# Decay sums of a state-space branch: clamped differences per head on VectorE and ScalarE, in place of two GpSimd passes and two VectorE passes

## The chip, the cores and the metric

The kernel runs on one core of a Trainium2 chip. The metric is the device time of one execution in microseconds (us); less is better. The core's engines each work through a queue of their own in order: TensorE (PE in the profile, with PEld for its weight loads), VectorE (DVE), ScalarE (ACT), GpSimd (POOL) and SyncE (SP), which issues the transfers of the weights. An instruction whose semaphore has not come holds up everything behind it on its engine, and nothing else.

## The reference, cut to what matters

The layer has a half-step feed-forward block, then two mixers side by side (a chunked state-space branch and a sparse attention branch), a memory cross-attention and a second half-step feed-forward block, for 256 tokens of 1024 features in float32. The change is in the state-space branch. With l = 128 tokens in a chunk, two chunks and 16 heads it computes

```
def segsum(a):
    l = a.shape[-1]
    cs = jnp.cumsum(a, axis=-1)
    diff = cs[..., :, None] - cs[..., None, :]
    mask = jnp.tril(jnp.ones((l, l), dtype=bool))
    return jnp.where(mask, diff, -jnp.inf)
...
    a = (dt * a_head.reshape(g, r)).transpose(0, 3, 4, 1, 2)
    decay_in = jnp.exp(segsum(a))
    cb = jnp.einsum('bclgn,bcsgn->bcgls', cmat, bmat)
    y_diag = jnp.einsum('bcgls,bgrcls,bcsgrp->bclgrp', cb, decay_in, xdt)
```

Since a is negative, a difference that survives the mask is at most 0. The kernel clamps every difference to at most 0, takes the exponential, and zeroes what the mask drops.

## The kernel before

**Tiles.** `E[tb]`, one for each chunk `tb`, holds for every head h the 128 x 128 differences: partition s, column (h, l), so 128 partitions x 2048 columns. `cs` holds the running sums, one column for each chunk and head. Products are made in a split float32 form: each piece of weights (128 x 1024) comes by a transfer of SyncE into one of 4 buffers `raw`, ScalarE writes its rounded high half `whi` (L150), and VectorE, for some pieces GpSimd, writes the rest `wlo` (L151); both have 6 buffers, so a cast waits until TensorE is done with the piece six before.

**Making E.** `ssd_decay` gets the sums with one small product (L548), turns them over (L555), writes them to DRAM (L560) and reads them back to all partitions with two transfers from GpSimd's queue (L562). GpSimd then subtracts `cs` from the whole of `E[tb]` (L563). Later, in `ssd`, VectorE clamps the whole of `E[tb]` to at most 0 (L599), ScalarE takes the exponential in halves of 8 heads (L604), VectorE multiplies by the masked products of C and B (L606), and TensorE uses the result as weights (L622).

**What runs beside it.** `fly` (L122) weaves generators together by counting TensorE's work: `ssd_decay`, `latent`, `xbc` and `k_index` share the first stretch. `xbc` (L433) makes 8 units of two 128-column blocks: TensorE fills a PSUM bank `ps_mm` from two weight pieces, ScalarE starts a block (L454), VectorE adds three shifted products (L456, "the convolution" below), ScalarE applies the silu (L458), and for the units that come last TensorE turns the block `wa` over (L120) into a bank `ps_t`, which ScalarE copies out (L443). The turns stand in TensorE's queue between the products, so a late silu stops all the products behind it. `k_index` turns over the index keys as well; ScalarE and VectorE split them into `kidxh` and `kidxl`. The second stretch weaves `dsa` (L653), `ssd` and `fill_mixers`; in it `dsa` adds up the index scores in `acc` on VectorE (L695).

**What sets the order.** The order on each engine is laid down when the program is built, by a scheduler that goes by its own estimates of the durations and may move an instruction ahead of others that wait; `issue_after` holds some instructions back behind a named one. Nothing is reordered on the chip.

Of the kernel before, what the change touches and what calls it, by code (L numbers as in the profile page):

```python
# [21 lines left out]
AF = mybir.ActivationFunctionType  # L22
ALU = mybir.AluOpType
AX = mybir.AxisListType

P = 128
T = 256
NTB = 2
# [4 lines left out]
H = 16  # L33
# [17 lines left out]
class Layer:  # L51
# [481 lines left out]

    def ssd_decay(self):

        nc = self.nc
        hb = lambda i: self.hv[:, None, i * H:(i + 1) * H].to_broadcast([P, NTB, H])
        dt = self.dtr
        nc.vector.tensor_tensor(dt, dt, hb(0), op=ALU.add)
        self.softplus(dt.rearrange("p a b -> p (a b)"), NTB * H)  # L540
        ea = self.small([P, H], "ea", bufs=1)
        nc.scalar.activation(ea, self.hv[:, H:2 * H], AF.Exp)
        dA = self.small([P, NTB, H], "dA", bufs=1)
        nc.vector.scalar_tensor_tensor(dA, dt, -1.0, ea[:, None, :].to_broadcast([P, NTB, H]),
                                       op0=ALU.mult, op1=ALU.mult)
        yield 14.0
        csp = self.psum("t")[:, :NTB * H]
        self.mm(csp, self.triu, dA.rearrange("p a b -> p (a b)"))  # L548
        cs = self.cs = self.small([P, NTB, H], "cs", bufs=1)
        nc.vector.tensor_copy(cs, csp.rearrange("p (a b) -> p a b", b=H))  # L550
        yield 1.5
        csT_p = self.psum("t")
        csT = self.small([P, T], "wa", bufs=4)[:H].rearrange("p (a b) -> p a b", b=P)
        for tb in range(NTB):
            self.transpose(csT_p[:H, tb * P:(tb + 1) * P], cs[:, tb, :])  # L555
        nc.vector.tensor_copy(csT, csT_p[:H, :T].rearrange("p (a b) -> p a b", b=P))
        scr = self.dp.tile([NTB, H * P], F32, name="cs_rows")
        self.E = []
        for tb in range(NTB):
            nc.gpsimd.dma_start(scr[tb].rearrange("(h l) -> h l", l=P), csT[:, tb, :])  # L560
            e = self.big((7, 9)[tb], F32, (P, H, P), "E")
            nc.gpsimd.dma_start(e.rearrange("p h l -> p (h l)"), scr[tb].partition_broadcast(P))  # L562
            nc.gpsimd.tensor_tensor(e, e, cs[:, tb, :].unsqueeze(2).to_broadcast([P, H, P]), op=ALU.subtract)  # L563
            self.E.append(e)

    def ssd(self, zs, xtok, bc, yT):

        nc = self.nc
        cs, E, dt, dskip = self.cs, self.E, self.dtr, self.hv[:, 2 * H:3 * H]
# [2 lines left out]
        S0, xe = sx[:, 0, :], sx[:, 1, :]  # L572
        dte, ecs = (self.small([P, H], tag, bufs=1) for tag in ("dte", "ecs"))
        with self.tc.issue_after(self.last_silu.ins):
            nc.scalar.activation(dte, E[0][:, :, P - 1], AF.Exp)
            nc.scalar.activation(ecs, cs[:, 1, :], AF.Exp)
        bcast = lambda v, n: v.unsqueeze(2).to_broadcast([P, n, HD])
        hview = lambda v: v.rearrange("p (h d) -> p h d", d=HD)
# [11 lines left out]
        for tb in range(NTB):  # L590
            ts = slice(tb * P, (tb + 1) * P)
            e = E[tb]
            cb = self.psum("t").rearrange("p (g c) -> p g c", c=P)
            for g in range(G):
                self.mm(cb[:, g, :], bc[:, g, ts], bc[:, 4 + g, ts])
            cbm = self.small([P, G, P], "w2b", bufs=2)
            nc.vector.tensor_tensor(cbm, cb, self.triu[:, None, :].to_broadcast([P, G, P]), op=ALU.mult)
            with self.tc.issue_after(self.last_conv.ins):
                nc.vector.tensor_scalar(e, e, 0.0, None, op0=ALU.min)  # L599
            yield 0.0  # L600
            for half in range(2):
                hs = slice(half * 8, half * 8 + 8)
                with self.tc.issue_after(self.last_silu.ins):
                    nc.scalar.activation(e[:, hs, :], e[:, hs, :], AF.Exp)  # L604
                ev = e[:, hs, :].rearrange("p (g r) l -> p g r l", g=2)
                nc.vector.tensor_tensor(ev, ev, cbm[:, 2 * half:2 * half + 2, :].unsqueeze(2).to_broadcast(  # L606
                    [P, 2, H // G, P]), op=ALU.mult)
            yield SSD_US[tb]
# [6 lines left out]
        for tb in range(NTB):  # L615
            ts = slice(tb * P, (tb + 1) * P)
            e, yt = E[tb], xtok[:, tb, :]
            for half in range(2):
# [6 lines left out]
                if tb == 1:  # L625
                    po = self.psum("mm")
                    for g in (2 * half, 2 * half + 1):
# [3 lines left out]
                                            op=ALU.mult)  # L631
# [9 lines left out]
            for g in range(G):  # L641
                nc.scalar.activation(yt[:, g * 256:(g + 1) * 256], yt[:, g * 256:(g + 1) * 256], AF.Copy,
                                     scale=rs[:, g:g + 1])
# [434 lines left out]
```

## Time and profile before

| | |
|---|---|
| median of 3 runs | 815.67 us (815.64 to 818.44) |
| the profiled execution: its own time | 814.78 us |
| its span, first to last instruction | 812.9 us |
| TensorE (PE) busy | 789.4 us, 97% of the span |
| VectorE (DVE) busy | 592.4 us, 73% |
| ScalarE (ACT) busy | 448.4 us, 55% |
| GpSimd (POOL) busy | 68.2 us, 8% |
| mean granted TensorE clock | 0.988 |

TensorE is busy nearly all the time, so a time can change in two ways only: by the stretches in which TensorE waits, and by those in which it runs at the lower of its two clocks (1.2 in place of 2.4 GHz, shown as a granted clock of 0.5). The shares of the other engines are means over stages of different kinds and tell little: it matters where they are late for TensorE.

### The profile page before, as it was taken

To read this page: it belongs to the slowest core of one execution; us is meant where nothing else is said; L and a number is where in the kernel's file an instruction comes from. 1 tells how busy PE (TensorE), PEld (TensorE's weight loads), DVE (VectorE), ACT (ScalarE), POOL (GpSimd) and SP (SyncE) were. 2 spreads that over 40 slices of the span, in tenths; PEclk is the share of its full clock that TensorE was granted. 3 is DMA by queue.
4 is the path that set the end of the run, shared out by engine and by line. 5 is a ranking of instruction groups with operands and counts; after the bars stand their busy time and mean duration, and the time that the engine had idled before them with its cause. 6 is when DMAs were issued, how large, how long until landed. Compare 5 with 4: busy or idle time off the path is not lost.

```text
span 812.9 us, 13145 instructions
## 1 busy us (share of the span) xinstructions
PE 789.4 (97%) x5070; PEld 717.5 (88%) x5070; DVE 592.4 (73%) x960; ACT 448.4 (55%) x782; POOL 68.2 (8%) x69
## 2 busy tenths in 40 slices
PE   8999999999989998989999999999999999999996
PEld 5888888887889997989999998899988988888885
DVE  4868776448588989698889767965659777776445
ACT  5756565433476684477667644544444666565330
POOL 1100000000032451230000000200002000000000
PEclk9999999999999999799999999999999999999999
DMA  7876555553656621236444456574433755555531
GB/s 249 271 267 224 193 182 194 187 200 104 210 189 228 208 74 51 81 108 233 165 150 135 158 175 215 170 276 161 156 120 134 256 191 195 192 184 194 192 105 53
DMA packets 39919, 142.90 MB, mean 176 GB/s; under 512 B 4592, under 2 KB 4896, under 8 KB 39472
## 3 DMA queue, kind: packets, MB, share of 16 engines
q1 hardware_dynamic: 38016, 134.63, 49.4%
q0 software_dynamic: 1840, 7.43, 2.9%
q8 instruction: 40, 0.66, 0.3%
q14 instruction: 23, 0.19, 0.1%
HBM read 140.97 MB, written 1.06 MB: 175 GB/s over the span
## 4 chain that ended last, share of the span: by engine, by line
PE 74%; DVE 11%; issue 8%; ACT 4%; DMA 2%; POOL 1%; SPq 0%; DVEq 0%; ACTq 0%; POOLq 0%
PE ps_mm L116 69%; DVE wlo L151 3%; PE ps_t L116 2%; PE ps_t L120 2%; DMA raw<-in_ffn_in_dram 2%; ACT whi L150 1%; PE ps_s L116 1%; DVE acc L695 1%; DVE acc L702 1%; DVE wa L456 1%; DVE m L701 1%; DMA raw<-in_w_pssd_dram 0%; POOL rstd L289 0%; DVE kv L794 0%; DVE kv L793 0%
## 5 line engine op out<-in xcount | busy, mean ns | idle before, releaser
L151 DVE TENSOR_TENSOR wlo<-raw,whi 128x1024 fp32r<-128x1024 f32 (+2 forms) x245 | 301.0, 1231 | 129.1 <-ACT whi L150 125.1
L150 ACT CAST whi<-raw 128x1024 fp32r<-128x1024 f32 (+2 forms) x253 | 263.2, 1044 | 188.1 <-PE ps_mm L116 124.6
L116 PE MATMUL ps_mm<-x1T,whi 128*128 128x256 f32 x768 | 143.9, 288 | 0.0
L116 PE MATMUL ps_mm<-x0T,whi 128*128 128x512 f32 x352 | 123.7, 400 | 2.9 <-ACT whi L150 2.1
L116 PEld LDWEIGHTS ps_mm<-x1T,whi 128*128 128x128 f32 x768 | 122.3, 195 | 0.0
L116 PE MATMUL ps_mm<-x1T,wlo 128*128 128x256 f32 x384 | 110.2, 287 | 0.0
L116 PE MATMUL ps_mm<-x3T,whi 128*128 128x512 f32 x304 | 105.6, 392 | 0.0
L116 PE MATMUL ps_mm<-x0T,wlo 128*128 128x256 f32 x352 | 97.0, 282 | 0.3 <-DVE wlo L151 0.3
L116 PE MATMUL ps_mm<-x3T,wlo 128*128 128x256 f32 x304 | 85.1, 280 | 0.0
L116 PEld LDWEIGHTS ps_mm<-x0T,whi 128*128 128x128 f32 x352 | 65.8, 188 | 20.6 <-ACT whi L150 3.6
L116 PEld LDWEIGHTS ps_mm<-x1T,wlo 128*128 128x128 f32 x384 | 75.1, 195 | 0.0
L116 PEld LDWEIGHTS ps_mm<-x3T,whi 128*128 128x128 f32 x304 | 56.9, 187 | 12.4
L116 PEld LDWEIGHTS ps_mm<-x0T,wlo 128*128 128x128 f32 x352 | 65.7, 189 | 1.6 <-DVE wlo L151 1.4
L116 PE MATMUL ps_mm<-whi,ah 128*128 128x512 f32 x154 | 60.2, 391 | 0.0
L116 PE MATMUL ps_mm<-wlo,ah 128*128 128x512 f32 x154 | 60.1, 390 | 0.0
L116 PE MATMUL ps_mm<-whi,al 128*128 128x512 f32 x154 | 59.9, 389 | 0.0
L116 PEld LDWEIGHTS ps_mm<-x3T,wlo 128*128 128x128 f32 x304 | 57.5, 189 | 0.0
L289 POOL TENSOR_TENSOR rstd<-rstd,mhalf 128x1 f32<-128x1 f32 (+1 forms) x12 | 11.3, 941 | 537.0 <-DVE rstd L288 537.0
L177 DVE TENSOR_TENSOR wa<-wa,ps_mm 128x256 f32<-128x256 f32 x82 | 34.0, 418 | 30.2 <-ACT wa L176 30.1
L347 ACT ACTIVATE wa<-wa 128x256 f32<-128x256 f32 x41 | 17.1, 417 | 48.1 <-DVE wa L177 48.1
L116 PEld LDWEIGHTS ps_mm<-whi,al 128*128 128x128 f32 x154 | 28.9, 188 | 6.2
L116 PEld LDWEIGHTS ps_mm<-whi,ah 128*128 128x128 f32 x154 | 29.0, 188 | 5.6
(296 smaller groups left out, 1551.5 us busy)
## 6 DMA issues: line engine op xcount, KB each, us to landing
raw<-in_ffn_in_dram SPq DMA_DIRECT2D x87, 512.0 KB, 4.1
raw<-in_ffn_out_dram SPq DMA_DIRECT2D x44, 512.0 KB, 3.5
raw<-in_w_xbc_dram SPq DMA_DIRECT2D x16, 512.0 KB, 4.3
raw<-in_w_gate_dram SPq DMA_DIRECT2D x16, 512.0 KB, 3.4
raw<-in_w_z_dram SPq DMA_DIRECT2D x8, 512.0 KB, 3.6
raw<-in_w_qidx_dram SPq DMA_DIRECT2D x8, 512.0 KB, 3.9
raw<-in_w_q_dram SPq DMA_DIRECT2D x8, 512.0 KB, 3.5
raw<-in_w_pssd_dram SPq DMA_DIRECT2D x8, 512.0 KB, 4.6
```

The costliest lines, as they stand in the source:

```text
L116: self.nc.tensor.matmul(out, a, b, start=start, stop=stop)
L120: self.nc.tensor.transpose(out, in_, self.ident)
L150: self.nc.scalar.copy(hi, src)
L151: (engine or self.nc.vector).tensor_sub(lo, src, hi.bitcast(F32))
L177: self.nc.vector.tensor_add(out, out, ps[:, :T])
L289: self.nc.gpsimd.tensor_tensor(v, v, self.mhalf[:, :n], op=ALU.pow)
L347: nc.scalar.activation(sg, self.join(gate, sg), AF.Silu)
L456: self.last_conv = nc.vector.scalar_tensor_tensor(v[:, d:], src[:, :T - d], cw[:, 3 - d:4 - d], v[:, d:], op0=ALU.mult, op1=ALU.add)
L695: nc.vector.scalar_tensor_tensor(acc[:, s], rl[:, s], self.widx[:, tb, h:h + 1], prev[:, s], op0=ALU.mult, op1=ALU.add)
L701: nc.vector.max(m8, acc[:, s])
L702: nc.vector.match_replace(out=acc[:, s], in_to_replace=m8, in_values=acc[:, s], imm_value=KILL)
```

## The change

The two GpSimd passes over E (L563) and the two VectorE clamps over E (L599) go. In their place each head of each chunk gets an instruction of its own over 128 columns: heads 0 to 7 on VectorE, as subtract and minimum in one; heads 8 to 15 on ScalarE, as relu(cs - E), which is the clamped difference with its sign turned. The exponentials of the second half of the heads therefore take the scale -1, and `dte` is made by two small instructions in place of one. The generator waits 12 us of counted TensorE work after the transfers and then issues the 32 instructions.

```
             nc.gpsimd.dma_start(e.rearrange("p h l -> p (h l)"), scr[tb].partition_broadcast(P))
-            nc.gpsimd.tensor_tensor(e, e, cs[:, tb, :].unsqueeze(2).to_broadcast([P, H, P]), op=ALU.subtract)
             self.E.append(e)
+        yield 12.0
+        for tb in range(NTB):
+            for h in range(H // 2):
+                nc.vector.tensor_scalar(self.E[tb][:, h, :], self.E[tb][:, h, :], cs[:, tb, h:h + 1], 0.0,
+                                        op0=ALU.subtract, op1=ALU.min)
+            for h in range(H // 2, H):
+                nc.scalar.activation(self.E[tb][:, h, :], self.E[tb][:, h, :], AF.Relu, scale=-1.0,
+                                     bias=cs[:, tb, h:h + 1])
+            yield 6.0
...
-            nc.scalar.activation(dte, E[0][:, :, P - 1], AF.Exp)
+            for half in range(2):
+                hs = slice(half * 8, half * 8 + 8)
+                nc.scalar.activation(dte[:, hs], E[0][:, hs, P - 1], AF.Exp, scale=(1.0, -1.0)[half])
...
-            with self.tc.issue_after(self.last_conv.ins):
-                nc.vector.tensor_scalar(e, e, 0.0, None, op0=ALU.min)
...
-                    nc.scalar.activation(e[:, hs, :], e[:, hs, :], AF.Exp)
+                    nc.scalar.activation(e[:, hs, :], e[:, hs, :], AF.Exp, scale=(1.0, -1.0)[half])
```

Buffer numbers shift between the two programs: `wa_2517` and `wa_2523` of before are `wa_2515` and `wa_2521` of the change, `whi_2691` with its `wlo_2692` is `whi_2705` with `wlo_2706`, and E's chunks are `E_2415` (first) and `E_2419` or `E_2418` (second).

**VectorE, in the middle of `xbc`.** Before, the convolution of two blocks with a weight split between and behind them:

```order
L456 SCALAR_TENSOR_TENSOR wa_2517<-ps_mm_2456,feat,wa_2517 128x255
L456 SCALAR_TENSOR_TENSOR wa_2517<-ps_mm_2456,feat,wa_2517 128x254
L456 SCALAR_TENSOR_TENSOR wa_2517<-ps_mm_2456,feat,wa_2517 128x253
L151 TENSOR_TENSOR wlo_2795<-raw_2793,whi_2794 128x1024
L456 SCALAR_TENSOR_TENSOR wa_2523<-ps_mm_2456,feat,wa_2523 128x255
L456 SCALAR_TENSOR_TENSOR wa_2523<-ps_mm_2456,feat,wa_2523 128x254
L456 SCALAR_TENSOR_TENSOR wa_2523<-ps_mm_2456,feat,wa_2523 128x253
```

The same place in the changed program, where two more rows of E stand a few rows ahead, among the last two rows of the convolution of `bcT_2097`:

```order
L456 SCALAR_TENSOR_TENSOR wa_2515<-ps_mm_2454,feat,wa_2515 128x255
L568 TENSOR_SCALAR E_2415<-E_2415,cs_2352 128x128
L456 SCALAR_TENSOR_TENSOR wa_2515<-ps_mm_2454,feat,wa_2515 128x254
L568 TENSOR_SCALAR E_2415<-E_2415,cs_2352 128x128
L456 SCALAR_TENSOR_TENSOR wa_2515<-ps_mm_2454,feat,wa_2515 128x253
L568 TENSOR_SCALAR E_2415<-E_2415,cs_2352 128x128 x4
L568 TENSOR_SCALAR E_2418<-E_2418,cs_2352 128x128 x6
L456 SCALAR_TENSOR_TENSOR wa_2521<-ps_mm_2454,feat,wa_2521 128x255
L568 TENSOR_SCALAR E_2418<-E_2418,cs_2352 128x128
L456 SCALAR_TENSOR_TENSOR wa_2521<-ps_mm_2454,feat,wa_2521 128x254
L568 TENSOR_SCALAR E_2418<-E_2418,cs_2352 128x128
L456 SCALAR_TENSOR_TENSOR wa_2521<-ps_mm_2454,feat,wa_2521 128x253
```

All 16 rows of E on VectorE stand ahead of the last convolution row of `wa_2521`, and the weight splits that stood here have moved behind them.

**ScalarE, at the same place.** Before:

```order
L454 ACTIVATE bcT_2097<-ps_mm_2371,feat 128x256
L150 CAST whi_2691<-raw_2690 128x1024
L454 ACTIVATE wa_2517<-ps_mm_2456,feat 128x256
L458 ACTIVATE bcT_2097<-bcT_2097 128x256
L150 CAST whi_2794<-raw_2793 128x1024
L458 ACTIVATE wa_2517<-wa_2517 128x256
L454 ACTIVATE wa_2523<-ps_mm_2456,feat 128x256
L150 CAST whi_2800<-raw_2799 128x1024
L454 ACTIVATE wa_2590<-ps_mm_2529,feat 128x256
L458 ACTIVATE wa_2523<-wa_2523 128x256
```

In the changed program:

```order
L571 ACTIVATE E_2415<-E_2415,cs_2352 128x128 x2
L454 ACTIVATE wa_2515<-ps_mm_2454,feat 128x256
L571 ACTIVATE E_2415<-E_2415,cs_2352 128x128 x2
L458 ACTIVATE bcT_2097<-bcT_2097 128x256
L571 ACTIVATE E_2415<-E_2415,cs_2352 128x128 x4
L150 CAST whi_2705<-raw_2704 128x1024
L458 ACTIVATE wa_2515<-wa_2515 128x256
L454 ACTIVATE wa_2521<-ps_mm_2454,feat 128x256
L571 ACTIVATE E_2418<-E_2418,cs_2352 128x128 x5
L454 ACTIVATE wa_2604<-ps_mm_2527,feat 128x256
L571 ACTIVATE E_2418<-E_2418,cs_2352 128x128
L458 ACTIVATE wa_2521<-wa_2521 128x256
```

Eight rows of E come ahead of the cast `whi_2705`, and six more ahead of the silu of `wa_2521`; the casts that followed stand behind that silu, and no table load is added.

**GpSimd, from E's transfers on.** Before:

```order
L562 DMA E_2415<-cs_rows 128x2048
L562 DMA E_2419<-cs_rows 128x2048
L563 TENSOR_TENSOR E_2415<-E_2415,cs_2352 128x2048
L151 TENSOR_TENSOR wlo_2692<-raw_2690,whi_2691 128x1024
L563 TENSOR_TENSOR E_2419<-E_2419,cs_2352 128x2048
L580 TENSOR_TENSOR xdt_2935<-xtok_2096,dtr_2002 128x1024 x2
```

In the changed program:

```order
L561 DMA cs_rows<-wa_2409 16x128 x2
L563 DMA E_2415<-cs_rows 128x2048
L563 DMA E_2418<-cs_rows 128x2048
L151 TENSOR_TENSOR wlo_2706<-raw_2704,whi_2705 128x1024
L591 TENSOR_TENSOR xdt_2965<-xtok_2096,dtr_2002 128x1024 x2
```

The weight split stays on GpSimd and now stands alone between E's transfers and `xdt`. TensorE's order is the same up to the products of `ssd` with E (some 50 us later), where groups of a few rows change places; SyncE's order is the same throughout.

## Rows read from the trace of the kernel before

**Rows 1.** The page, busy time of each engine over the span.

```profile
span 812.9 us, 13145 instructions
PE 789.4 (97%) x5070; PEld 717.5 (88%) x5070; DVE 592.4 (73%) x960; ACT 448.4 (55%) x782; POOL 68.2 (8%) x69
```

**Rows 2.** Stretches: length, busy PE, PEld, DVE, ACT, POOL, then clock, DMA.

```profile
252.00:276.00 24.00, 24.00 (x203) 23.97 (x202) 20.80 (x30) 14.77 (x25) 14.52 (x8) 1.00 0.67 245
312.00:316.00 4.00, 4.00 (x24) 4.00 (x23) 3.94 (x6) 1.30 (x3) 0.00 (x0) 0.57 0.40 131
```

**Rows 3.** Timeline of PE: start, length; in brackets idle time and releaser.

```profile
270.02 0.60 PE L120 MATMUL ps_t<-ident,wa 128*128 128x128 f32 x4
...
277.39 0.44 PE L120 MATMUL ps_t<-ident,wa 128*128 128x128 f32 x2 [0.80 <-ACT wa L458]
...
283.51 0.44 PE L120 MATMUL ps_t<-ident,wa 128*128 128x128 f32 x2 [0.46 <-ACT xtok L443]
...
310.56 0.39 PE L116 MATMUL ps_s<-kidxh,w2a 128*128 128x256 f32 x1 [2.58 <-ACT wa L692]
```

**Rows 4.** Timeline of POOL, around E's transfers and around xdt.

```profile
257.28 1.08 POOL L562 DMA_DIRECT2D E<-cs_rows  x2 [2.60 <-DMA cs_rows<-wa]
262.81 3.61 POOL L563 TENSOR_TENSOR E<-E,cs 128x2048 f32<-128x2048 f32 x1 [4.44 <-DMA E<-cs_rows]
266.39 3.38 POOL L151 TENSOR_TENSOR wlo<-raw,whi 128x1024 fp32r<-128x1024 f32 x1
269.73 4.59 POOL L563 TENSOR_TENSOR E<-E,cs 128x2048 f32<-128x2048 f32 x1
291.76 4.67 POOL L580 TENSOR_TENSOR xdt<-xtok,dtr 128x1024 f32<-128x1024 f32 x2 [17.43 <-ACT xtok L443]
...
294.53 1.90 POOL L580 TENSOR_TENSOR xdt<-xtok,dtr 128x1024 f32<-128x1024 f32 x1
```

**Rows 5.** The tile E, from 250 to 275 us: transfers, issue to landing.

```profile
DMA to landing us min/median/max: 5.5/6.9/8.4
```

**Rows 6.** Timeline of DVE, from the convolutions of xbc to the first index scores.

```profile
259.67 1.22 DVE L151 TENSOR_TENSOR wlo<-raw,whi 128x1024 fp32r<-128x1024 f32 x1
260.81 1.51 DVE L456 SCALAR_TENSOR_TENSOR bcT<-ps_mm,feat,bcT 128x255 f32<-128x255 f32 x3
...
265.42 2.08 DVE L151 TENSOR_TENSOR wlo<-raw,whi 128x1024 fp32r<-128x1024 f32 x1 [0.90 <-ACT whi L150]
267.42 1.50 DVE L456 SCALAR_TENSOR_TENSOR wa<-ps_mm,feat,wa 128x255 f32<-128x255 f32 x3
268.84 2.01 DVE L151 TENSOR_TENSOR wlo<-raw,whi 128x1024 fp32r<-128x1024 f32 x1
...
272.19 3.21 DVE L151 TENSOR_TENSOR wlo<-raw,whi 128x1024 fp32r<-128x1024 f32 x1
...
283.39 0.42 DVE L151 TENSOR_TENSOR kidxl<-ps_t,kidxh 128x256 fp32r<-128x256 f32 x1
...
291.57 1.23 DVE L599 TENSOR_SCALAR E<-E 128x2048 f32<-128x2048 f32 x1
...
296.04 0.68 DVE L668 SCALAR_TENSOR_TENSOR w2a<-ps_mm,w2a 64x512 fp32r<-64x512 f32 x1 [1.95 <-ACT w2a L667]
```

**Rows 7.** Timeline of ACT at the same place.

```profile
261.46 1.06 ACT L150 CAST whi<-raw 128x1024 fp32r<-128x1024 f32 x1 [0.73 <-PE ps_mm L116]
262.41 0.56 ACT L454 ACTIVATE wa<-ps_mm,feat 128x256 f32<-128x256 f32 x1
...
269.02 0.42 ACT L458 ACTIVATE wa<-wa 128x256 f32<-128x256 f32 x1 [0.24 <-DVE wa L456]
```

**Rows 8.** Groups by shape, DVE and ACT: count, busy us, mean ns of one.

```profile
L726 DVE TENSOR_SCALAR wa<-wa,asum 128x128 f32<-128x128 f32 x16 | 4.5, 280 | 0.0
L737 ACT COPY wc<-ps_t 128x128 f32<-128x128 f32 x16 | 4.2, 264 | 3.5 <-DVE w2d L151 3.2
L722 ACT ACTIVATE wa<-wa,amax 128x128 f32<-128x128 f32 x16 | 6.2, 390 | 0.0
```

**Rows 9.** Timeline at 236 us: a small DVE chain while POOL works.

```profile
235.84 2.72 DVE L529 SCALAR_TENSOR_TENSOR spp<-spp,spq 128x32 f32<-128x32 f32 x3
235.88 2.41 POOL L151 TENSOR_TENSOR wlo<-raw,whi 128x1024 fp32r<-128x1024 f32 x1 [2.99 <-ACT whi L150]
```

## The prediction

> **What bounds the kernel now.** I read the page first: TensorE is busy 789.4 of 812.9 us [rows 1], so the change can only act through TensorE's waits and its clock. Next the stretches around E: from 252 to 276 us TensorE is busy 24.00 of 24 us at full clock [rows 2]. Nothing can be gained there, only lost. Then TensorE's timeline. Behind 276 us it waits twice for a turn of a block `wa`: 0.80 us at 277.39 for a silu and 0.46 us at 283.51 [rows 3]. The turns at 270.02 go through without a wait. Further on stands the wait of 2.58 us that ends at 310.56, and behind it 4 us at a mean clock of 0.57 [rows 2, 3], which cost 4 x 0.43 = 1.7 us of full-speed work. The reader should see that 1.26 us of waits stand near the change and some 4.3 us twenty to thirty us later. The tile's users come last: GpSimd starts on E at 262.81, when the first transfer lands [rows 4]; the transfers are issued at 257.3 and, half a row later, at 257.8, and the second lands after 8.4 us [rows 4, 5], so at 266.2.
>
> **What is removed.** GpSimd loses 3.61 and 4.59 us [rows 4]. Nobody waits for these directly, but VectorE's weight splits suffer under them: one takes 1.22 us at 259.67 and 2.08, 2.01 and 3.21 us while GpSimd works [rows 6], together 3.6 us lost. VectorE loses two clamps of some 1.23 us [rows 6]. These give nothing: at 296.04, right behind them, VectorE has stood idle 1.95 us for ScalarE's `w2a` [rows 6], and ScalarE has the same exponentials to make ahead of it as before (plus one of 8 columns for `dte`). So the start of the index scores keeps its distance from TensorE.
>
> **What is added.** The nearest VectorE row is the multiplication by a per-partition scalar at 128 x 128: 280 ns [rows 8]. Starts overlap: a split of 1.22 us is followed after 1.14 us [rows 6], so 0.08 us goes off: 0.20 us each, 16 x 0.20 = 3.2 us; without overlap 4.5 us. ScalarE: the nearest row has a per-partition bias at 128 x 128, 390 ns; a copy without one takes 264 ns [rows 8]. A cast of 1.06 us is followed after 0.95 us [rows 7], so I take 0.30 us each, 16 x 0.30 = 4.8 us, between 0.16 (the copy with overlap) and 0.39. Both are below the 8.2 us that GpSimd needed, but GpSimd had nothing to do and these two engines feed TensorE.
>
> **Where they lie.** VectorE comes to its first row of E after one convolution row, at 260.81 + 0.5 = 261.3 [rows 6], ScalarE at 261.46 - 0.73 = 260.7 [rows 7]. E lands at 262.8, so both stand still, 1.5 and 2.1 us; what is queued behind are the convolutions of `bcT_2097` and the cast `whi_2705`. From 262.8 ScalarE does four rows of E (1.2), an L454 (0.46, the distance left by its 0.56 us), a silu (0.33) and four rows of E (1.2): the cast starts at 266.0 and ends at 266.95, against 262.5 before [rows 7]. That by itself costs nothing: its piece is used by TensorE only behind the turns at 277.39. GpSimd's split follows at 267.0; alone it takes 2.41 us [rows 9], so until 269.4, about where it ended before, 266.39 + 3.38 = 269.8 [rows 4]; the transfer waiting for its `raw` buffer is not late.
>
> VectorE meanwhile, from 262.8, with convolution rows at (268.84 - 267.42) / 3 = 0.47 us [rows 6]: five convolution rows and four of E until 266.0, four more of E until 266.8, and then the second chunk, which has landed. Here GpSimd's split begins. **Do rows of E wait for it?** A chain of three small VectorE instructions that starts at 235.84 takes 2.72 us against a GpSimd split of 2.41 us begun 0.04 us later [rows 9]: VectorE was held until GpSimd ended. Those instructions read two tensors from SBUF. The rows of E read one. But the clamp, one tensor of SBUF too, started at 291.57, and `xdt` on GpSimd, started at 291.76, took 294.53 - 291.76 = 2.77 us for its first piece, 0.87 us more than the 1.90 us of its second [rows 4, 6]: the clamp kept GpSimd out until 292.80. Between free and held I take held, since this form of instruction is the one that was seen to exclude GpSimd. The Trainium skill ("SBUF — State Buffer", section "Who interferes with whom") says the same more sharply: a VectorE `tensor_scalar` in its two-port mode and a GpSimd instruction exclude each other for the whole instruction, and the one that starts first wins. The 0.87 us agrees with it for one order of the two; no row here shows the other. By that rule the sum is the one that follows; without it, it is the first rival's.
>
> Held, the order is: about one row of the second chunk done at 267.0, five more from 269.4 to 270.4, then three convolution rows and two of E, 1.8 us: `wa_2521` is convolved at 272.2. If GpSimd gets in only when the burst of E ends at 268.0, it holds the next row of E until 270.4 and the last convolution row ends at 271.75. I take 272.0. Its silu follows until about 272.4. TensorE wants that block 0.2 us behind 270.02 [rows 3], so **it waits about 2.2 us where it waited for nothing.** Before, this silu ran at 269.02 [rows 7], so the cover that is used up was about 0.8 us.
>
> **What is late next.** Between that convolution and the split of `kidxl`, for which the turn at 283.51 waits along with its copy [rows 3, 6], VectorE has 13 convolution rows and, as the splits moved behind, 6 splits in place of 5: 13 x 0.47 + 6 x 1.14 = 13.0 us. I add 1.0 us for casts that come late, since ScalarE's rows of E delay them by a few tenths each (0.5 to 2.0). So `kidxl` starts at 272.0 + 14.0 = 286.0. Before it started at 283.39 [rows 6], 14.5 us behind the same convolution (268.84), of which 2.8 us were the two held splits. The shift is 2.6 us, and the turn moves from 283.51 to about 286.1. Between the two, the wait of 0.80 us at 277.39 disappears: that silu is done near 277.7 and TensorE comes at about 278.8. From here TensorE works on as before, everything is started by it or by engines in the same order, and the shift stays to the end: the removed clamps lie where VectorE waits anyway.
>
> **The sum.** +2.2 (first turns) - 0.8 (second) + about 1.7 - 0.5 (the turn at 283.51) = +2.6 us. Against the profiled execution that is 814.78 + 2.6 = 817.4 us. The median shown is 815.67, 0.9 us above that execution, so I forecast 818.2 us, 0.3% above. Bounds: with 0.28 us a row on VectorE and 0.39 on ScalarE, some 14 and 9 rows ahead of the first late turn add at most 1.1 + 0.8 us; with the shorter rows GpSimd's split starts earlier by as much as VectorE gains, and the late turn stays within 0.3 us. With 0.5 to 2.0 us of late casts this case runs from +1.5 to +5, so 817 to 820.5.
>
> **Rivals.**
> *The rows of E are not held (VectorE and GpSimd pass each other).* For it: convolutions at 267.42, which read PSUM and one tensor of SBUF, took 0.47 us each while GpSimd worked [rows 4, 6]. Against it: the 0.87 us above. Then `wa_2521` is convolved at 269.9, TensorE waits 0.3 us at the first turns, and `kidxl` starts at 269.9 + 14.0 = 283.9, 0.5 us late: 815.67 + 0.3 = 816 us, no change.
> *Faster: the 2.58 us wait at 310.56 goes, with the slow stretch behind it* [rows 2, 3]. For it: two clamps, 2.45 us of VectorE, leave just ahead of the chain that ends there. Against it: the 1.95 us idle at 296.04 [rows 6]. It decides if VectorE's chain comes 2.6 us earlier relative to TensorE. Price: -2.58 - 1.7 = -4.3 us, 811.4 us; with the two turns' waits as well (-1.3) 810.1 us.
> *Slower than forecast: the clock.* A wait of 2.58 us was followed by 4 us at 0.57 [rows 2, 3]. The new wait of 2.2 us may do the same, but its loss falls into the slack ahead of the turn at 283.51. If the clock falls behind that later turn instead, 1.7 us come on top, and each us by which E's second chunk lands later (8.4 us is one sample) stops VectorE and ScalarE at once: 2.6 + 1.7 + 1 = +5.3, 821 us.
>
> **How the numbers follow.** Held rows, 817 to 820.5: 0.50. Not held: 0.20. Clock or a late transfer: 0.16. The later wait goes: 0.14. About 0.5%, 4.1 us, is what a measurement of this kernel can tell from no change. Slower by more: the third case and a small part of the first, 0.20. Faster by more: 0.13. Within: 0.67. The range 812 to 822 us leaves out most of the fast case and the end of the slow one.
>
> **What would show it.** On VectorE, rows of E of about 0.28 us, and one or a few of about 2.4 us at 267 to 270.5 beside GpSimd's split: if none is long, the first rival holds. On ScalarE, rows of about 0.39 us. On TensorE, a wait of about 2 us ahead of the turns near 272.4 and none at the next ones, then one at about 286. Splits of 1.22 us all through 265 to 275. VectorE idle for `w2a` by about 2 us near 298, and the long wait still there near 313. I am wrong if TensorE passes 284 us without having lost 2 us, or if the long wait changes by more than 1 us.

## The result and the profile after

The changed kernel takes 822.23 us, median of six runs (821.37 to 827.48), against 815.65 us for the kernel before on the same chip: 6.6 us or 0.8% more. The ratio on record for the two is 1.0105, 95% interval [1.0076, 1.0134], higher than the 1.0081 of the two medians; runs of the same kernel in other comparisons gave 1.0095 and 1.0109. It is slower, and outside the forecast range by 0.2 us. The profiled execution is the slowest of the six (827.48 us), so its waits are larger than a typical run's; a second and a third profile stand among the experiments.

The stretch answers to [rows 2 to 7]. First the tile E after the change: durations in ns, least, median and largest, and the landing of the two transfers.

```profile
L571 ACT ACTIVATE E<-E,cs x16: 386/392/403, 267.8 to 277.4; 128x128 f32<-128x128 f32 x16
L568 DVE TENSOR_SCALAR E<-E,cs x16: 270/278/2396, 267.8 to 276.0; 128x128 f32<-128x128 f32 x16
...
DMA to landing us min/median/max: 9.0/10.7/12.4
```

The same transfers that landed after 5.5 and 8.4 us [rows 5] now took 9.0 and 12.4. The timelines of VectorE, ScalarE and GpSimd show what that does to the queues:

```profile
267.82 0.29 DVE L568 TENSOR_SCALAR E<-E,cs 128x128 f32<-128x128 f32 x1 [5.02 <-DMA E<-cs_rows]
...
271.75 3.38 DVE L568 TENSOR_SCALAR E<-E,cs 128x128 f32<-128x128 f32 x6 [0.30 <-DMA E<-cs_rows]
...
290.87 0.41 DVE L151 TENSOR_TENSOR kidxl<-ps_t,kidxh 128x256 fp32r<-128x256 f32 x1
...
303.25 0.68 DVE L677 SCALAR_TENSOR_TENSOR w2a<-ps_mm,w2a 64x512 fp32r<-64x512 f32 x1 [3.11 <-ACT w2a L676]
```

```profile
267.82 0.70 ACT L571 ACTIVATE E<-E,cs 128x128 f32<-128x128 f32 x2 [5.58 <-DMA E<-cs_rows]
...
276.78 0.42 ACT L458 ACTIVATE wa<-wa 128x256 f32<-128x256 f32 x1 [1.83 <-DVE wa L456]
```

```profile
258.77 1.09 POOL L563 DMA_DIRECT2D E<-cs_rows  x2 [2.57 <-DMA cs_rows<-wa]
272.11 2.34 POOL L151 TENSOR_TENSOR wlo<-raw,whi 128x1024 fp32r<-128x1024 f32 x1 [12.26 <-ACT whi L150]
```

VectorE stands 5.0 us and ScalarE 5.6 us in front of their first rows. One row of E lasts 2.396 us, beside the split of weights that GpSimd starts at 272.11. TensorE, which answers to [rows 3]:

```profile
272.35 0.44 PE L120 MATMUL ps_t<-ident,wa 128*128 128x128 f32 x2 [0.65 <-ACT wa L458]
...
277.25 0.69 PE L120 MATMUL ps_t<-ident,wa 128*128 128x128 f32 x2 [4.47 <-ACT wa L458]
...
316.78 0.39 PE L116 MATMUL ps_s<-kidxh,w2a 128*128 128x256 f32 x1 [1.66 <-ACT wa L701]
...
367.01 0.35 PE L116 MATMUL ps_s<-kv,w2e 128*128 128x256 f32 x1 [0.94 <-DVE w2e L677]
...
368.69 0.39 PE L116 MATMUL ps_mm<-x1T,wlo 128*128 128x256 f32 x1 [1.33 <-DVE wlo L151]
...
395.80 0.39 PE L116 MATMUL ps_mm<-w2d,w2c 128*128 128x256 f32 x1 [1.64 <-DVE w2d L151]
```

The reader should see two places: 5.1 us of waits at the turns, and, some ninety to a hundred and twenty microseconds on, waits of 0.94, 1.33 and 1.64 us that wait for no row of E. To size both, three stretches are cut at the same events in every kernel: **A** from the issue of E's transfers to the split of `kidxl`, **B** from there to the last of the passes on VectorE that pick the top scores out of `acc` (the top-k passes), **C** from there to the copy of the second keys and values into `kidxl`. Windows of A, B and C, after, then before (columns as in [rows 2]):

```profile
258.80:290.90 32.10, 26.96 (x211) 26.32 (x209) 25.30 (x50) 21.18 (x48) 3.40 (x3) 0.89 0.56 205
290.90:363.40 72.50, 68.36 (x507) 67.02 (x506) 60.10 (x123) 44.92 (x88) 19.13 (x10) 0.91 0.24 81
363.40:449.60 86.20, 81.60 (x649) 80.41 (x648) 75.25 (x156) 57.41 (x134) 4.12 (x4) 0.96 0.46 155
```

```profile
257.30:283.40 26.10, 24.95 (x208) 24.51 (x206) 23.95 (x34) 17.16 (x32) 12.58 (x5) 1.00 0.69 250
283.40:357.00 73.60, 69.90 (x519) 68.61 (x520) 63.12 (x125) 45.63 (x89) 21.59 (x10) 0.91 0.26 87
357.00:436.90 79.90, 77.02 (x638) 75.96 (x638) 72.41 (x156) 56.70 (x134) 4.14 (x4) 1.00 0.47 160
```

Products move across the cuts (638 against 649 in C), so lengths alone mislead. The table therefore gives TensorE's **loss**: its idle time, plus its busy time times (1 - granted clock), added up from windows of some 2 us. Length minus loss of A, B and C together is 165 to 167 us in all seventeen profiles, so the loss accounts for the differences to within some 1.5 us. Behind C every kernel takes 376.0 to 376.2 us. The landing is that of E's two transfers; "own time" is that of the one profiled execution, the ratio that of the timed runs to runs of the kernel before beside them on the same chip.

| run | ratio [95%] | own time | landing | A | B | C |
|---|---|---|---|---|---|---|
| kernel before | 1 | 814.78 | 5.5/8.4 | 1.1 | 10.4 | 2.9 |
| changed, first profile | 1.0105 [1.0076, 1.0134] | 827.48 | 9.0/12.4 | 6.8 | 10.8 | 7.9 |
| again | 1.0095 [1.0070, 1.0121] | 821.09 | 7.6/10.7 | 5.1 | 11.0 | 4.3 |
| again_b | 1.0109 [1.0068, 1.0150] | 822.55 | 8.4/11.5 | 6.6 | 7.4 | 8.2 |
| split_behind | 1.0099 [1.0067, 1.0130] | 822.74 | 7.3/10.8 | 6.2 | 7.4 | 8.4 |
| split_later | 1.0109 [1.0076, 1.0141] | 825.96 | 8.7/11.8 | 6.9 | 9.2 | 8.2 |
| no_pool_split | 1.0072 [1.0048, 1.0096] | 819.19 | 6.2/9.3 | 1.0 | 7.6 | 8.3 |
| wait_only | 1.0062 [1.0039, 1.0085] | 819.99 | 6.8/10.3 | 2.2 | 7.6 | 8.1 |
| work_only | 1.0031 [1.0012, 1.0051] | 817.68 | 5.9/9.0 | 0.4 | 9.0 | 8.1 |
| scalar_later | 1.0023 [1.0001, 1.0045] | 816.82 | 7.1/10.4 | 3.9 | 4.4 | 6.7 |
| vector_later | 1.0065 [1.0039, 1.0091] | 824.46 | 8.6/11.8 | 3.5 | 12.1 | 7.7 |
| two_units_later | 0.9923 [0.9903, 0.9942] | 810.59 | 8.4/11.5 | 0.4 | 5.2 | 3.2 |
| late_order | 1.0001 [0.9978, 1.0023] | 813.69 | 7.8/11.1 | 0.5 | 6.2 | 7.4 |
| early_order5 | 1.0019 [0.9996, 1.0042] | 814.13 | 8.1/11.2 | 5.7 | 7.6 | 0.9 |
| before_order | 1.0073 [1.0048, 1.0097] | 821.39 | 6.5/9.8 | 1.9 | 11.0 | 7.4 |
| before_order5 | 0.9975 [0.9950, 0.9999] | 814.50 | 7.9/11.0 | 3.1 | 8.6 | 1.3 |
| two_units_order5 | 0.9925 [0.9898, 0.9952] | 809.51 | 6.5/9.9 | 0.0 | 8.2 | 1.2 |

Against the first profile before, A loses 4.0 to 5.7 us more in the changed kernel, and C 1.4 to 5.5. But that profile has the earliest landing of all, and the kernel before pays for a late one as well. Two programs of the experiments, before_order and before_order5, have its order on every engine up to 330 us; with landings of 9.8 and 11.0 us in place of 8.4, A loses 1.9 and 3.1 us in place of 1.1. From before_order5, the tile E, then TensorE's turns:

```profile
DMA to landing us min/median/max: 7.9/9.4/11.0
```

```profile
272.43 0.44 PE L120 MATMUL ps_t<-ident,wa 128*128 128x128 f32 x2 [1.30 <-ACT wa L458]
...
280.28 0.44 PE L120 MATMUL ps_t<-ident,wa 128*128 128x128 f32 x2 [1.45 <-ACT wa L458]
```

Beside its 3.1 us at 11.0, the changed kernel's 5.1 us at 10.7 and 6.6 at 11.5 are 2.0 to 3.5 us more, not 4.0 to 5.7.

The experiments ask for the cause of each. Their expectations name theories: by the stall, landing and burst theories the cost lies in the stop for E's transfers and the rows that follow it at once; by the held-row theory, in the row of E that GpSimd's split holds; by the later theory, in C.

### The profile page after: what moved, and what is told of

Same layout as the page of the kernel before. It is cut to its first block, busy times and chain, and to the rows that moved or that the text cites. A ratio compares the mean times of both kernels' runs of the same rounds, so it can differ in the third digit from the quotient of the medians.

```text
span 825.8 us, 13166 instructions
## 1 busy us (share of the span) xinstructions
PE 795.6 (96%) x5070; PEld 723.5 (88%) x5070; DVE 593.6 (72%) x974; ACT 452.8 (55%) x799; POOL 57.4 (7%) x67
## 4 chain that ended last, share of the span: by engine, by line
PE 74%; DVE 12%; issue 5%; DMA 4%; ACT 4%; POOL 0%; SPq 0%; DVEq 0%; ACTq 0%; POOLq 0%
PE ps_mm L116 69%; DVE wlo L151 3%; PE ps_t L120 2%; PE ps_t L116 2%; DMA raw<-in_ffn_in_dram 2%; DVE acc L704 2%; DMA E<-cs_rows 2%; PE ps_s L116 1%; ACT whi L150 1%; DVE acc L711 1%; DMA raw<-in_w_q_dram 1%; DVE m L710 1%; DVE E L568 0%; DVE E L615 0%; DVE w2e L677 0%
## 5 line engine op out<-in xcount | busy, mean ns | idle before, releaser
L151 DVE TENSOR_TENSOR wlo<-raw,whi 128x1024 fp32r<-128x1024 f32 (+2 forms) x245 | 297.6, 1218 | 133.7 <-ACT whi L150 130.1
```

The lines of the kernel that those rows point to most:

```text
L151: (engine or self.nc.vector).tensor_sub(lo, src, hi.bitcast(F32))
```

## Experiments at the rows of E (stretch A)

**again** and **again_b** are the changed kernel once more (823.75 and 823.36 us).

> The changed kernel once more, for a second profiled execution. Stall theory (the rows of E stand early in the in-order queues of VectorE and ScalarE, both stop until the two 1 MB transfers of E have landed, and the landing varies): 820 to 824 us, the second transfer lands 8 to 13 us after its issue, and the time lost by the last convolution of the stretch follows the landing. Held-row theory (one row held 2.4 us by GpSimd's split is most of the loss): the same time, also where the landing is as early as 8.4 us. Later theory (half of the loss arises behind 346 us): again about 5 us lost between 360 and 400 us, as in the first profile.

> The changed kernel beside the other three on the same chip, and a third profile of it: 821 to 825 us. Landing theory: the wait at the turns and the lost clock up to the first kidx split follow the landing of E, 5.1 and 1.7 us with landings of 9.0 and 12.4 us, 3.5 and 1.6 us with 7.6 and 10.7 us.

Stretch A follows the landing only loosely: 5.1 us at 7.6/10.7, 6.2 at 7.3/10.8, 6.6 at 8.4/11.5. The later theory's 5 us stood in C in one profile of the two, again_b; in again C lost 1.4 us more than before.

**wait_only** keeps one row for each engine and transfer; **work_only** keeps all rows but lets them wait for no transfer. (All exponentials take the scale 1 in both.)

```
-            for h in range(H // 2):
+            for h in (0,):
...
-            for h in range(H // 2, H):
+            for h in (H // 2,):
```

> Leaves out 28 of the 32 rows: one row of each transfer stays on VectorE and one on ScalarE at the same place, so the waits for the two landings stay and the work goes (the output is not the reference's). Stall theory: at least 4 of the 6.6 us stay, 819.5 to 822 us. Held-row theory: GpSimd's split meets only single rows, most of the loss goes, 815.5 to 817.5 us. Later theory: the order behind the rows is that of the changed kernel, so 3 us or more stay behind 346 us, 819 us or more.

```
-                nc.vector.tensor_scalar(self.E[tb][:, h, :], self.E[tb][:, h, :], cs[:, tb, h:h + 1], 0.0,
+                nc.vector.tensor_scalar(rows[:, 0, :], self.triu, cs[:, tb, h:h + 1], 0.0,
...
-                nc.scalar.activation(self.E[tb][:, h, :], self.E[tb][:, h, :], AF.Relu, scale=-1.0,
+                nc.scalar.activation(rows[:, 1, :], self.triu, AF.Relu, scale=-1.0,
```

> All 32 rows are made of a constant 128x128 block and written to a spare tile, so they wait for no transfer; the exponentials read E as it landed (the output is not the reference's). Stall theory: no stop, 8 us of rows spread over two engines that have room, 814.5 to 817.5 us. Held-row theory: rows still run beside GpSimd's splits, 817.5 us or more. Later theory: 819 us or more.

820.05 and 818.52 us. With the waits and two rows on each engine A loses 2.2 us at a landing of 10.3, about what the kernel before loses at such a landing (1.9 at 9.8, 3.1 at 11.0). With all rows it is 5.1 to 6.8. (With the rows gone, the builder also laid some weight splits and casts earlier.) So the stop costs most when a burst of rows comes behind it, ahead of the convolutions and silus.

work_only says less than it was made for. Without the wait the builder put the rows elsewhere: VectorE's run from 250.1 to 267.4 us, ScalarE's from 251.0 to 264.6, one by one among the other work, so there is no burst. Spread like this they cost nothing that can be seen (0.4 us in A), though one of them was held by GpSimd's split too:

```profile
264.63 3.01 DVE L569 TENSOR_SCALAR acc<-triu,cs 128x128 f32<-128x128 f32 x4
```

Both runs still lose 8.1 us in C, so what happens at E's rows does not explain all of the change.

**scalar_later** and **vector_later** put one engine's sixteen rows behind the sixth unit's last silu or convolution.

```
+        yield "rows"
+        for tb in range(NTB):
+            with self.tc.issue_after(self.last_silu.ins):
+                for h in range(H // 2, H):
+                    nc.scalar.activation(self.E[tb][:, h, :], self.E[tb][:, h, :], AF.Relu, scale=-1.0,
```

> The changed kernel with ScalarE's sixteen rows of E put behind the last SiLU that stands when the sixth of the eight units is done; VectorE's sixteen stay early. Burst theory (in the changed kernel a queue stops until E lands and then has its rows to make in one go: about 4 us of stop and 6.2 us of rows on ScalarE, 4 us and 4.5 us on VectorE, and the SiLUs behind come that much too late for TensorE; ScalarE is the one that decides): from E's issue to the end of the top-k passes 95 to 99 us in place of 102.5, the whole 817.5 to 820 us. If VectorE decides: 821.5 us or more, and 101 us or more to the end of the top-k passes. Held-row theory: the held row stays, 822 us or more. Later theory: the stretch from the end of the top-k passes to the second set of keys and values (77.7 us before, 81.3 in the second profile of the changed kernel) stays over 81 us in any case, since the order there is the changed kernel's.

> The mirror image: VectorE's sixteen rows of E put later, ScalarE's stay early. Burst theory with ScalarE deciding: 821 to 824 us and 101 us or more from E's issue to the end of the top-k passes. If VectorE decides, or the held row: 817 to 820 us and under 100 us there. Later theory: over 81 us from the end of the top-k passes to the second set of keys and values, as the order there is the changed kernel's.

817.08 and 820.49 us. By what was expected ScalarE would decide: from E's issue to the end of the top-k passes it took 93.0 and 102.6 us. But in A the two are alike: it loses 3.9 us with VectorE's rows early and 3.5 with ScalarE's, so either queue keeps half or more of the 5.1 to 6.8 us. A silu needs the convolution from one queue and its place in the other, which would explain it; no run shows more. The difference between the two lies in B (4.4 against 12.1), most of it TensorE's clock, where the later rows stand at 292 us in both and TensorE's order differs as well; and vector_later's profiled execution is one of its two slowest.

**no_pool_split**, **split_behind**, **split_later** ask what the held row costs.

```
-            for _ in self.a_steps(ps, t["w_xbc"][u], xT, u % 2 == 1):
+            for _ in self.a_steps(ps, t["w_xbc"][u], xT, u in (5, 7, 1)):
```

> The changed kernel with the one split of weights by GpSimd that ran beside the rows of E given to VectorE (1.2 us more on VectorE, 2.4 less on GpSimd). Held-row theory: no row takes over 0.4 us and the time falls by 1 to 3 us, 820 to 822.5 us. Burst theory: the row of 2.4 us goes, but VectorE has as much work in its place, 822 to 824.5 us.

821.01 us, A down to 1.0. But this edit also moves one of TensorE's turns a few products back, and the landing was early (9.3), so it doesn't settle the question. The next two leave the split on GpSimd and put a small copy ahead of it:

```
+                one = self.small([P, 1], "one", bufs=1)
+                last = self.nc.gpsimd.tensor_copy(one, self.E[1][:, 7, 0:1])
+                with self.tc.issue_after(last.ins):
+                    self.split(raw, hi, lo, self.nc.gpsimd)
```

> The changed kernel with one tiny copy on GpSimd that reads VectorE's last row of E ahead of the split of weights that held a row; the split so runs behind the rows, and the orders on TensorE, VectorE and ScalarE are the changed kernel's, row for row. Held-row theory: no row over 0.4 us, 2.1 us of VectorE come back ahead of the late SiLU, TensorE's wait at the turn falls by up to 2 us and the time by 1.5 to 3 us against the changed kernel in the same call. Landing theory (the stop for E's transfers alone decides): within 1 us of it.

It missed: the copy read E as it landed, ahead of the second block's rows, and a row was held as before (2.407 us). So this is one more run of the changed kernel (822.74 us). In **split_later** the copy reads a block convolved behind the rows (`self.mark[:, 0:1]`).

> The second try at the held row: the tiny copy on GpSimd now reads the convolution block that follows the rows of E on VectorE, so GpSimd's split of weights runs behind the rows. TensorE's order is the changed kernel's row for row; on VectorE one split of weights and one convolution, both behind the rows, change places with their neighbours. Held-row theory: no row of E over 0.4 us, TensorE's wait at the turn 1.5 to 2.5 us less than the 3.5 to 4.3 us of the changed kernel's profiles, the time 1.5 to 3 us less than 823.4. Landing theory: within 1 us of 823.4, since ScalarE's rows end last anyway (274.6 us against VectorE's 273.2 in the third profile).

The tile E and TensorE's timeline in split_later:

```profile
L576 DVE TENSOR_SCALAR E<-E,cs x16: 275/279/287, 266.8 to 272.7; 128x128 f32<-128x128 f32 x16
...
DMA to landing us min/median/max: 8.7/10.3/11.8
```

```profile
271.27 0.44 PE L126 MATMUL ps_t<-ident,wa 128*128 128x128 f32 x2 [0.28 <-ACT wa L464]
274.24 0.69 PE L126 MATMUL ps_t<-ident,wa 128*128 128x128 f32 x2 [2.52 <-ACT wa L464]
286.88 0.44 PE L126 MATMUL ps_t<-ident,wa 128*128 128x128 f32 x2 [0.15 <-ACT wa L464]
290.39 0.44 PE L126 MATMUL ps_t<-ident,wa 128*128 128x128 f32 x2 [1.16 <-ACT xtok L449]
```

No row is held, and the first turns wait 2.8 us in place of 4.3 (again_b, with a landing 0.3 us earlier). Yet the later turns wait 1.3 us that again_b does not, and the time is 824.81 us, no better. So undoing the hold by a later split gives no time back. What the hold alone costs isn't shown: by the first turns it can be up to 1.5 us, and the later split may have cost as much. In work_only a held row cost nothing that can be seen.

**two_units_later** makes both halves of the change later.

```
-        yield 12.0
+        yield "rows"
...
+            with self.tc.issue_after(self.last_conv.ins):
...
+            with self.tc.issue_after(self.last_silu.ins):
...
+            if u == 1:
+                self.done.add("rows")
```

> The whole change, but the rows of the first block are put behind the last convolution of the sixth of the eight units, and those of the second block further back, when both transfers have long landed. Stall theory: neither engine waits for a transfer any more, 815 to 818 us. Held-row theory: the place is behind GpSimd's last split in this stretch, so the held row goes too, 816 to 819 us; this run does not tell the two apart, but both from the later theory, which says 820 us or more.

810.04 us: faster than the kernel before by 5.9 us, which no theory had. E landed as late as in again_b (8.4/11.5 in both), and A lost 0.4 us in place of 6.6. So a late landing costs nothing where no queue stands waiting for it. Against the kernel before, most of the gain in the profiles stands in B (5.2 us lost in place of 10.4), all of it by TensorE's clock; why the clock held there isn't shown. VectorE's rows and splits in this run:

```profile
273.56 1.22 DVE L151 TENSOR_TENSOR wlo<-raw,whi 128x1024 fp32r<-128x1024 f32 x1
276.12 1.65 DVE L571 TENSOR_SCALAR E<-E,cs 128x128 f32<-128x128 f32 x8
277.68 1.22 DVE L151 TENSOR_TENSOR wlo<-raw,whi 128x1024 fp32r<-128x1024 f32 x1
```

Eight rows take 1.65 us and no split is held.

## Experiments on the order behind the top-k passes (stretch C)

Where C begins, the two programs differ on VectorE, though the edit is far away. Before (instructions in order):

```
L668 SCALAR_TENSOR_TENSOR w2e_3494<-ps_mm_3432,w2e_3494 64x512
L231 SCALAR_TENSOR_TENSOR yTl_2786<-ps_t_3499,feat,yTh_2785 128x128
L231 SCALAR_TENSOR_TENSOR yTl_2786<-ps_t_3512,feat,yTh_2785 128x128
L718 SCALAR_TENSOR_TENSOR wa_3679<-acc_2791,ps_s_3674 128x384
```

Changed:

```
L677 SCALAR_TENSOR_TENSOR w2e_3523<-ps_mm_3461,w2e_3523 64x512
L231 SCALAR_TENSOR_TENSOR yTl_2816<-ps_t_3528,feat,yTh_2815 128x128
L231 SCALAR_TENSOR_TENSOR yTl_2816<-ps_t_3541,feat,yTh_2815 128x128
L151 TENSOR_TENSOR wlo_3723<-raw_3721,whi_3722 128x1024
L231 SCALAR_TENSOR_TENSOR yTl_2816<-ps_t_3528,feat,yTh_2815 128x128
L231 SCALAR_TENSOR_TENSOR yTl_2816<-ps_t_3541,feat,yTh_2815 128x128
L727 SCALAR_TENSOR_TENSOR wa_3708<-acc_2821,ps_s_3703 128x384
```

A split of weights and two rows of `yTl` now stand ahead of the first row of the softmax (L718, now L727), and further rows change places behind, on ScalarE and TensorE too. The three profiles of the changed kernel have the same order, row for row, on every engine, so the order is the program's. What TensorE waited for in C in the kernel before (us in total, times, longest), then in again_b:

```profile
PE ps_s L116 <- DVE w2a L668: 1.2, 1, 1.2
PE ps_t L120 <- DVE yTl L231: 0.9, 1, 0.9
PE ps_mm L116 <- DVE w2d L151: 0.5, 2, 0.3
```

```profile
PE ps_mm L116 <- DVE w2d L151: 1.9, 2, 1.6
PE ps_mm L116 <- DVE wlo L151: 1.3, 1, 1.3
PE ps_s L116 <- DVE w2e L677: 1.0, 1, 1.0
```

Here `w2a` and `w2e` are the split queries that meet the keys `kv`, and `w2d` is the low part of the softmax turned over. From TensorE's timeline in again_b:

```profile
360.11 0.74 PE L116 MATMUL ps_s<-kv,w2a 128*128 128x256 f32 x4 [0.36 <-DVE w2a L677]
...
362.05 0.35 PE L116 MATMUL ps_s<-kv,w2e 128*128 128x256 f32 x1 [0.96 <-DVE w2e L677]
...
363.73 0.39 PE L116 MATMUL ps_mm<-x1T,wlo 128*128 128x256 f32 x1 [1.32 <-DVE wlo L151]
...
390.89 0.39 PE L116 MATMUL ps_mm<-w2d,w2c 128*128 128x256 f32 x1 [1.64 <-DVE w2d L151]
```

and its clock behind these waits (windows):

```profile
364.00:368.00 4.00, 4.00 (x23) 4.00 (x23) 2.56 (x9) 1.97 (x7) 0.00 (x0) 0.57 0.37 133
...
390.00:394.00 4.00, 2.62 (x12) 2.42 (x13) 3.69 (x9) 3.50 (x8) 0.00 (x0) 0.72 0.88 286
```

Over C it is 5.0 us of idle time and 3.2 us of clock; before, 2.9 and none. In again, with much the same waits (1.9, 1.3 and 0.5 us), the clock stayed at 1.00 in C, and C lost 4.3 us.

One constant of the plan, the wait of 3.0 ahead of the last four heads of the index scores (in `dsa`), turns VectorE's order at this place on and off. It also moves rows from 330 us on, among them some scores and turns on TensorE.

```
             else:
-                yield 3.0
+                yield 1.5
```

**late_order** is two_units_later with 1.5; **before_order** is the kernel before with 1.5. On VectorE the first 27 rows of C then stand as in the changed kernel.

> The version with the rows two units later (810.0 us) with one constant of the plan changed, 3.0 to 1.5 in the wait ahead of the last four heads of the index scores, which makes the program behind the top-k passes stand in the changed kernel's order on VectorE (a split of weights and two rows of yTl ahead of the first softmax). Later theory: the stretch from the end of the top-k passes to the second set of keys and values grows from 78 to 81 us or more and the time to 813 to 816 us. Burst and held-row theories, by which all of the loss lies at E's rows: 809 to 811 us.

> The kernel before, GpSimd's subtraction and the clamps in place, with the same constant at 1.5 in place of 3.0, which makes the program behind the top-k passes stand in the changed kernel's order. Later-order theory: 3 to 6 us slower than the kernel before, all of it behind the top-k passes, without a row of E changed. If all of the loss lies at E's rows: within 1 us of the kernel before.

815.49 us in place of 810.04, and 820.71 us against 813.96: the order that 1.5 gives costs 5 to 7 us without an instruction on E being changed. C loses 7.4 us in both. But it is not the same loss as in the changed kernel, though VectorE's rows stand alike. TensorE's waits in C in before_order:

```profile
PE ps_s L116 <- DVE w2a L668: 2.6, 1, 2.6
PE ps_s L116 <- DVE w2e L668: 1.1, 1, 1.1
PE ps_mm L116 <- ACT wc L737: 0.7, 1, 0.7
PE ps_mm L116 <- DVE wlo L151: 0.5, 1, 0.5
```

So these two runs show that an order alone can cost this much here. For the changed kernel the direct test is the other way round. **early_order5** is the changed kernel with 5.0, **before_order5** and **two_units_order5** the other two with 5.0. There C begins much as before, with the split behind the first reductions.

> The changed kernel, rows of E at its early place, with the wait of the plan ahead of the last four heads of the index scores at 5.0 in place of 3.0, which makes the first two dozen rows of VectorE behind the top-k passes stand much as in the kernel before (the first split of weights behind the first two reductions). Later-order theory: 2 to 5 us less than the changed kernel in the same call, taken behind the top-k passes, while the wait at the turns stays over 3 us. If all of the loss lies at E's rows: within 1 us of the changed kernel.

> The kernel before with the constant of the plan at 5.0 in place of 3.0, as the control for the two versions with 5.0. If the order that 5.0 gives is better for any kernel: 811 to 813 us. If it only gives the kernel before its own order back: 813.5 to 816 us.

> Rows of E two units later and the constant at 5.0: the first sixty rows of VectorE behind the top-k passes stand as in the kernel before with 5.0, so these two differ by the edit alone. If the edit at this place gains: 3 to 6 us less than the kernel before with 5.0 in the same call, 807 to 811 us. If the 5.9 us of the version with the rows later came from its order alone: no less than the kernel before with 5.0.

815.94, 813.99 and 809.58 us. With its early rows and 5.7 us of loss in A, the changed kernel comes back from 823.36 (again_b, beside it) to 815.94 us. C loses 0.9 us in place of 8.2, and the waits named above are gone (early_order5):

```profile
PE ps_s L116 <- DVE w2a L677: 0.4, 1, 0.4
PE ps_mm L116 <- DVE w2d L151: 0.2, 1, 0.2
PE ps_t L120 <- DVE yTl L231: 0.2, 1, 0.2
```

The same constant gives the kernel before only 1.4 us by the medians, 2.0 by the ratio. So about 5 us of what the change costs is its order behind the top-k passes (0.90% less 0.25%, give or take some 2 us by the spread of the runs). The ratios side by side:

| rows of E | order of before | order of the change | 5.0 |
|---|---|---|---|
| passes of before | 1 | 1.0073 | 0.9975 |
| per head, early (the change) | - | 1.0095 to 1.0109 | 1.0019 |
| per head, two units later | 0.9923 | 1.0001 | 0.9925 |

Down a column the order behind the top-k passes is held nearly fixed (in the middle one on VectorE, less so on TensorE): the edit at its place costs 0.2 to 0.4%, give or take as much by the intervals of the ratios, and two units later it gains 0.5 to 0.8%. Along a row, the order of the change costs 0.7 to 0.8% against that of before, and 0.8 to 1.0% against 5.0. The best kernels, two_units_later and two_units_order5, can't be told apart.

## Why the prediction was wrong

- **What bounds the kernel:** right. All of the change lies in TensorE's waits and clock.
- **The step that failed** is the last of "What is late next": "everything is started by it or by engines in the same order, and the shift stays to the end". The order is another one behind the top-k passes, and costs about 5 us there: the changed kernel laid out with 5.0 takes 815.94 us in place of 823.36, its loss in C is 0.9 us in place of 4.3 to 8.4, and the kernel before gains 1.4 to 2.0 us by the same constant. The change section had said that rows change places later; the sum gave it no term.
- **The landing:** taken as 5.5 and 8.4 us from one sample, 7.3 to 9.0 and 10.7 to 12.4 us in the changed kernel's profiles. The stops were 5.0 and 5.6 us in the first, in place of 1.5 and 2.1. The third rival had named it, at 1 us. Its 821 us stand near the 822.23, but by luck: it has no term for C.
- **Price of a row:** right. VectorE 278 ns, eight in 1.65 us, so (1.65 - 0.28) / 7 = 0.20 us from start to start; ScalarE 392 ns, 0.29 to 0.30 us from start to start.
- **Rows are held:** the event was right (2.396 us), its weight is open: with the split behind the rows the time is the same (split_later). The Trainium skill ("SBUF — State Buffer", "Who interferes with whom") states that of a VectorE instruction in its two-port mode and a GpSimd instruction the one that starts first blocks the other for the whole instruction. That row agrees with it, 2.396 us beside a split of 2.34; no run shows in which mode the row ran.
- **TensorE's wait:** 2.2 us was forecast near 272.4; 0.65 and 4.47 us came, and the clock fell beside it (1.7 us). Part of the excess goes with the landing, by which the kernel before loses more as well. That the wait at the next turn vanishes and splits take 1.22 us was right, and so was the stretch from the convolution of `wa_2521` to `kidxl`: 14.0 us forecast, 14.2 measured. The wait forecast for the turn after it, at about 286, did not come; TensorE had lost 6.8 us by then.
- **"The removed clamps give nothing":** in the changed kernel VectorE still stands for `w2a` (3.11 us), as forecast. The edit as a whole can gain, though: with the rows out of the transfers' way it gains 4 to 6 us. With the order at 5.0 on both sides the gain is in A: 3.1 us of loss become 0.0. How much of it comes from the clamps and how much from GpSimd's passes isn't shown.
- **The sum:** with the order held fixed the edit costs 0.0036 and 0.0044 of 814 us (before_order to again_b, before_order5 to early_order5), 2.9 and 3.6 us, each give or take some 3 to 4 us by the intervals of the ratios. That is near the 2.6 us forecast, as are the 2.0 to 3.5 us in A at like landings. But the terms are not those forecast: in A all of it stands at the first turns and in the clock beside them.
- **The wait at 310.56:** 1.66 us at 316.78 after, 0.9 less, inside the bound of 1 us. The fast rival did not happen in this kernel: B loses no less in this profile than before (10.8 and 10.4 us).

What stays open: why the order moved (the builder's estimates are in no trace), how much of C's cost is the split ahead of the softmax and how much the rows behind it, since the constant moves TensorE's rows too, what the held row costs alone, where two_units_later's gain in B comes from, and why B differs so much between executions of the same program. Placing the rows earlier than the transfers' worst landing but later than now was not tried.

## What to carry to other kernels

Where a scheduler lays out the program, an edit has two effects, its own and the new order's, and the second can be larger and lie far away: compare the orders to the end of the program, give each place that differs a term, and judge an edit between kernels whose order is the same elsewhere. Compare stretches that hang on a transfer at like landings, the kernel before included. An instruction that waits for a transfer belongs behind the latest landing seen, not the one in a single trace; on two queues that feed the same engine, a stop and a burst of work add up.

## What was not expected of the hardware

Two transfers of 1 MB, issued at the same place of the program, landed after 5.5/8.4 us in the profile with the earliest landing and 9.0/12.4 us in the one with the latest, and even the kernel before lost 1.1 to 3.1 us in A by it. And small waits need not be small for TensorE: in again_b waits of 0.36, 0.96 and 1.32 us between 360 and 364 us are followed by the window at a clock of 0.57 shown above, 4 x 0.43 = 1.7 us more. Not always: in again, waits of 0.55 and 1.32 us at the same place were followed by a clock of 1.00.
